# Page gathers spread thinner over the token tiles, feature tiles paced by attention units, output weights loaded by column halves

## The chip, the cores and the metric

The kernel runs on one core of one Trainium2 chip. TensorE (PE) multiplies matrices, VectorE (DVE), ScalarE (ACT) and GpSimd (POOL) work on tiles in on-chip memory, and SyncE (SP) does little but issue DMAs. ACT issues DMAs too, on a queue of its own: a DMA that ACT issues stands in ACT's instruction order like a cast does, and whatever stands behind it waits until the issue is through. The metric is the device time of one execution in microseconds (us); lower is better.

## The reference

One decoder layer on 1024 prompt tokens and 8 sample tokens, model width 1024. A combined projection feeds two groups of heads: a chunked gMLP (u, v, gate z_a; 512 wide) and a sparse attention (8 query heads, 2 key/value heads, three branches: compressed, selected, sliding window). Their outputs are concatenated, projected once, added to the input and normalised. For the sample tokens, part of the keys and values come out of paged caches.

```python
z = jnp.einsum('btd,de->bte', rms_norm(x, norm_g), w_in)
u, v, z_a, q, kc, vc, ks, vs, kw, vw, g, z_b = jnp.split(z, offs, axis=-1)
a_out, vn = gmlp_branch(u, v, z_a, ...)             # u * (W_s @ layer_norm(v) + b) * silu(z_a)
pages = lambda c: c[page_table].reshape(Bn, past, N_KV, HEAD_DIM)    # sample tokens only
kc_full = jnp.concatenate([pages(ck_cmp), kc], 1)   # likewise vc, ks, vs
kcc, starts = compress(kc_full, w_ck, pe_ck)
o_b = nsa_core(q, pos, gates, kcc, vcc, c_end, kb, vb, kw_all, vw_all, kwpos)
mix = jnp.concatenate([a_out, o_b * silu(z_b)], -1)
y = rms_norm(x + jnp.einsum('bte,ed->btd', mix, w_out), final_g)
```

## The kernel before

All large products are made with operands split into a high and a low part (`hi`, a cast by ACT, and `lo`, a subtraction by DVE or POOL), so that one product is three matmuls: hi·hi, lo·hi and hi·lo. Helper `f_mm` and its like issue them all from line L45, which is why the rows are told apart by tile names and not by lines.

The program runs in stages on one core:

- 0 to 60 us: the input is read and normalised, and the first three feature tiles are made. A **feature tile** (PSUM tile `pf`) is 128 columns of the projection for all 1032 tokens, 8 slices of the model width times 3 column thirds times 3 products.
- 60 to 97 us: the four **query tiles** (t = 0 to 3), also `pf`. Each takes two weight tiles, loaded by SP into `wst` (from `wF`), cast to `whi` by ACT (L143) and subtracted to `wlo` (L144). The weights of t = 0 and 1 are in the list `q_first`, made ahead; those of t = 2 and 3 are asked for inside the loop with `f_weights(8 + t)`.
- 97 to 180 us: eight **token tiles of v** (`ptv`), with the gate of the gMLP (`pg`).
- 180 to 226 us: eight token tiles of **keys** (`pta`), 199 to 243 us: eight token tiles of **values** (`ptb`), each evacuated by ACT from PSUM into `ka`, `kvc` or `vb`, `kvc`, then cast to `k` or `v`. PE then transposes `kvc` (`pct`) for the compressed branch.
- 246 to 365 us: compression (`Xh`, `pc`) and the sample tokens' attention, between which the remaining nine feature tiles are strewn as filler work.
- 365 to 735 us: 32 **attention units**, one for each of eight query blocks qb, two key/value heads and two halves. A unit has scores `S`, softmax on DVE, ACT and POOL (`Pl`, `Pw`), transposes `pt`, casts `th` and `tl` of the probabilities, and products with the values into `o`. For qb 0 to 3 the filler beside them is the rest of the feature tiles; for qb 4 to 7 it is the output projection `pout`, which needs `woh` and `wol`, the high and low parts of the output weights. These two reuse the memory of `xh` and `xl`, the input's parts, so they can be loaded only after the last feature tile.

What sets the order. A scheduler orders each engine's instructions by a time model of its own; `tc.high_priority(FILL)` with a negative FILL marks filler that yields to everything else, and `tc.issue_after(x)` keeps what it wraps behind instruction x. Each engine then runs its instructions in that fixed order.

Function `early(t, behind)` is called once for each of the 24 token tiles t: 0 to 7 are those of v, 8 to 15 of keys, 16 to 23 of values. It puts side work on ACT's DMA queue behind that tile's evacuation. For t under 16 it gathers one of 16 pages of `cg` (for compression, copied from cache to scratch memory), loads one half slice of the output weights (`wost`), casts it (`wohi`) and has POOL subtract (`wolo`), whose result the next call stores to `wol_d`. For t from 16 on it gathers two of 16 pages of `kg` (for selected attention). `cg` has the layout (o k) p c, with 256 rows of 128 elements on both sides; `kg` splits each row of the page in two, from "o p (k c)" to "(o k) p c" with k = 2. Each page is 128 KB.

After qb 3 is written (`od`), the output weights are loaded: SP issues eight loads of 128x1024 (L1189, pool `wop` with 7 buffers) and two of `wol` (L1193), and ACT casts eight slices of `woh` (L1190). `fg`, the last norm's weights, takes over the memory of `RS`.

Of the kernel before, what the change touches and what calls it, by code (L numbers as in the profile page):

```python
# [12 lines left out]
P = 128  # L13
# [26 lines left out]
def trunk(tc, io, outs):  # L40
# [7 lines left out]
    with ExitStack() as top:  # L48
# [251 lines left out]
        wp = wp_ctx.enter_context(tc.tile_pool(name="wp", bufs=9, reuse_waits="tile"))  # L300
        wr_ctx = ExitStack()
# [9 lines left out]
        W.update(pool=wp, rp=wr, raw=4, behind=sy.dma_start(Sq, io["Sq"]))  # L311
# [27 lines left out]
        for t in range(4):  # L339
            if t:  # L340
                qF = f_tiles(t + 1)
            wts = f_weights(8 + t) if t > 1 else q_first[t]
# [33 lines left out]

        def early(t, behind):
            half, k = t % 2, t // 2
            cs_ = slice(half * 512, half * 512 + 512)
            with tc.issue_after(behind.ins):  # L380
                if wo_low:
                    s.dma_start(*wo_low.pop())
                if t < 16:
                    s.dma_start(cg[:, :, t, :], io["cA"][bass.ds(prow[t], 1)].rearrange("o k p c -> (o k) p c"))
                    st = wo.tile([P, 512], F32, tag="wost", name="wost")
                    s.dma_start(st, io["w_out"][k, :, cs_])
# [5 lines left out]
                else:  # L392
                    for j in range(2 * t - 32, 2 * t - 30):
                        s.dma_start(kg[:, :, j, :],  # L394
                                    io["cB"][bass.ds(prow[j], 1)].rearrange("o p (k c) -> (o k) p c", k=2))
# [203 lines left out]
        def feature_tiles(bank):  # L599
# [5 lines left out]
            for n, (what, i, _) in enumerate(todo):  # L605
# [5 lines left out]
                for j in range(3):  # L611
                    ps = bank()("pf")[:, 0:CH]
                    for k in range(KT):
                        hi, lo = wts[k // 4]
                        c = (k % 4) * P
                        with tc.high_priority(FILL):
                            at_bank[1] = f_mm(hi[:, c:c + P], lo[:, c:c + P], [ps], k, (j,))
# [25 lines left out]
        at_bank = [0, None]  # L643
        banks = [ps_s, ps_b]
# [506 lines left out]
        for i, (qb, h, tp) in enumerate(todo):  # L1151
            units = [n_values(q) + 2 for q, _, _ in todo[i:] if (q < EARLY) == (qb < EARLY)]
# [25 lines left out]
            if qb == EARLY - 1:  # L1178
# [3 lines left out]
                fg = xp.tile([P, D], F32, tag="row", name="fg")  # L1182
# [3 lines left out]
                wop = wo_ctx.enter_context(tc.tile_pool(name="wop", bufs=7, side="right", reuse_waits="tile"))  # L1186
                for k in range(KT):
                    st = wop.tile([P, D], F32, tag="wost", name="wost")
                    sy.dma_start(st, io["w_out"][k])  # L1189
                    s.copy(woh[:, k, :], st)  # L1190
                    if k == 6:
                        for half in range(2):
                            sy.dma_start(f32(wol[:, :, half * 512:half * 512 + 512]), wol_d[half])  # L1193
# [130 lines left out]
```

## Time and profile before

| | us |
|---|---|
| median of 3 runs | 749.3 (747.53 to 750.55) |
| profiled execution | 745.39 |
| its span, first to last instruction | 743.6 |
| PE busy within the span | 683.4 |
| DVE busy | 510.6 |
| ACT busy | 383.0 |
| POOL busy | 294.5 |

The profiled execution took 1.8 us more than its span and is 3.9 us under the median of the runs. "Busy" leaves out DMA-issuing instructions, so ACT's 383.0 us do not hold the time its queue spends on issues; those are named ACTq in the rows (SPq for SyncE's). Matmul records overlap, so a matmul's pace is read from the distance of starts, or from the number that starts in a stretch.

The granted TensorE clock is a column of the stage table, 1.00 for full speed and 0.50 for half. It was 0.968 in the mean over the span.

### The profile page before, as it was taken

To read this page: it belongs to the slowest core of one execution; us is meant where nothing else is said; L and a number is where in the kernel's file an instruction comes from. 1 tells how busy PE (TensorE), PEld (TensorE's weight loads), DVE (VectorE), ACT (ScalarE), POOL (GpSimd) and SP (SyncE) were. 2 spreads that over 40 slices of the span, in tenths; PEclk is the share of its full clock that TensorE was granted. 3 is DMA by queue.
4 is the path that set the end of the run, shared out by engine and by line. 5 is a ranking of instruction groups with operands and counts; after the bars stand their busy time and mean duration, and the time that the engine had idled before them with its cause. 6 is when DMAs were issued, how large, how long until landed. Compare 5 with 4: busy or idle time off the path is not lost.

```text
span 743.6 us, 12579 instructions
## 1 busy us (share of the span) xinstructions
PE 683.4 (92%) x4186; PEld 628.1 (84%) x4186; DVE 510.6 (69%) x1470; ACT 383.0 (52%) x898; POOL 294.5 (40%) x282
## 2 busy tenths in 40 slices
PE   8998999998899256999999999979999999999994
PEld 6997988898799256898899999757989988988993
DVE  5836894798561135843299998968788789878743
ACT  7613422232453135512278777798567676676631
POOL 0034133646132104152322343558565565556421
PEclk9999899999999768999999999999999999999998
DMA  9333655333873245254542212955031121212011
GB/s 323 111 113 143 181 143 166 104 93 117 253 217 111 78 147 176 99 196 154 145 117 66 86 53 93 332 211 176 26 113 44 59 57 61 71 57 86 15 57 57
DMA packets 67945, 91.29 MB, mean 123 GB/s; under 512 B 5744, under 2 KB 45280, under 8 KB 67080
## 3 DMA queue, kind: packets, MB, share of 16 engines
q1 hardware_dynamic: 54344, 75.48, 31.7%
q10 hardware_dynamic: 13376, 12.85, 5.4%
q0 software_dynamic: 160, 2.15, 0.9%
q8 instruction: 33, 0.54, 0.3%
q14 instruction: 32, 0.26, 0.1%
HBM read 67.85 MB, written 28.91 MB: 130 GB/s over the span
## 4 chain that ended last, share of the span: by engine, by line
PE 54%; DVE 12%; DMA 11%; issue 7%; ACTq 6%; ACT 5%; POOL 3%; SPq 1%; POOLq 0%; DVEq 0%
PE pf L45 15%; PE pout L45 11%; PE o L45 8%; PE S L45 7%; PE pt L966 7%; ACTq L394 4%; DMA kg<-in_cB 2%; DMA zd<-z 2%; DMA wost<-in_w_out 1%; PE ptb L45 1%; PE po L45 1%; DVE sp L445 1%; PE pouts L45 1%; POOL vt L469 1%; PE pA L45 1%
## 5 line engine op out<-in xcount | busy, mean ns | idle before, releaser
L970 DVE TENSOR_TENSOR tl<-pt,th 128x512 fp32r<-128x512 f32 (+1 forms) x160 | 100.7, 643 | 25.6 <-ACT th L969 24.9
L45 PE MATMUL pf<-xh,whi 128*128 128x344 f32 x384 | 109.7, 332 | 4.8 <-ACT whi L143 2.5
L45 PE MATMUL pf<-xl,whi 128*128 128x344 f32 x384 | 111.1, 329 | 0.0
L45 PE MATMUL pf<-xh,wlo 128*128 128x344 f32 x384 | 110.1, 328 | 1.0 <-DVE wlo L144 1.0
L969 ACT CAST th<-pt 128x512 fp32r<-128x512 f32 (+1 forms) x160 | 84.8, 550 | 30.0 <-PE pt L966 27.2
L943 POOL TENSOR_TENSOR Pw<-Pw,r 128x640 f32<-128x640 f32 (+3 forms) x112 | 76.2, 699 | 42.8 <-DVE r L937 17.2
L45 PE MATMUL pout<-woh,mix 128*128 128x512 f32 (+1 forms) x272 | 86.4, 383 | 1.8 <-ACT mix L1003 1.8
L943 POOL TENSOR_TENSOR Pl<-Pl,r 128x384 f32<-128x384 f32 (+5 forms) x36 | 49.0, 1362 | 89.6 <-DVE r L937 33.9
L45 PEld LDWEIGHTS pf<-xh,whi 128*128 128x128 f32 x384 | 71.2, 195 | 6.7 <-ACT whi L143 3.2
L45 PE MATMUL o<-th,v 128*128 128x256 f32 x264 | 73.3, 298 | 3.0 <-ACT th L969 2.1
L45 PEld LDWEIGHTS pf<-xl,whi 128*128 128x128 f32 x384 | 71.8, 195 | 1.2 <-issue 1.0
L45 PEld LDWEIGHTS pf<-xh,wlo 128*128 128x128 f32 x384 | 71.2, 194 | 1.8 <-DVE wlo L144 1.4
L45 PE MATMUL o<-tl,v 128*128 128x256 f32 x264 | 69.3, 288 | 0.8 <-DVE tl L970 0.7
L45 PEld LDWEIGHTS pout<-woh,mix 128*128 128x128 f32 x272 | 49.9, 188 | 10.5 <-ACT mix L1003 2.0
L889 ACT ACTIVATE Pl<-Pl,nmx 128x128 f32<-128x128 f32 (+7 forms) x64 | 49.8, 778 | 15.1 <-DVE nmx L885 12.9
L45 PE MATMUL S<-kwS,q 128*128 128x384 f32 (+2 forms) x224 | 54.9, 336 | 2.9 <-DVE nmx L885 1.9
L929 ACT ACTIVATE Pw<-Pw,nmx 128x640 f32<-128x640 f32 (+4 forms) x64 | 44.5, 696 | 22.5 <-DVE nmx L921 20.6
L45 PEld LDWEIGHTS o<-th,v 128*128 128x128 f32 x264 | 49.8, 189 | 6.3 <-ACT th L969 2.9
L45 PE MATMUL S<-ksS,q 128*128 128x384 f32 (+5 forms) x192 | 53.5, 363 | 1.1 <-DVE nmx L885 0.7
L45 PEld LDWEIGHTS o<-tl,v 128*128 128x128 f32 x264 | 49.9, 189 | 3.8 <-DVE tl L970 2.6
L45 PE MATMUL pout<-wol,mix 128*128 128x512 f32 (+1 forms) x136 | 52.1, 384 | 0.0
L143 ACT CAST whi<-wst 128x512 fp32r<-128x512 f32 (+2 forms) x50 | 28.4, 587 | 41.1 <-DMA wst<-in_wTv 11.9
(338 smaller groups left out, 1674.3 us busy)
## 6 DMA issues: line engine op xcount, KB each, us to landing
q<-qd SPq DMA_DIRECT2D x32, 256.0 KB
wst<-in_wF SPq DMA_DIRECT2D x26, 256.0 KB
raw<-in_xw SPq DMA_DIRECT2D x7, 708.0 KB
wost<-in_w_out ACTq DMA_DIRECT2D x16, 256.0 KB
wol_d<-wolo ACTq DMA_DIRECT2D x16, 256.0 KB
wol<-wol_d SPq DMA_DIRECT2D x2, 2048.0 KB
wost<-in_w_out SPq DMA_DIRECT2D x8, 512.0 KB
xt<-in_x_prompt SPq DMA_DIRECT2D x8, 512.0 KB
```

Of the source, the lines that this page charges most:

```text
L45: return pe.matmul(out, lhsT, rhs, start=start, stop=stop, skip_group_check=True)
L143: s.copy(hi[:, :n], st[:, :n])
L394: s.dma_start(kg[:, :, j, :], io["cB"][bass.ds(prow[j], 1)].rearrange("o p (k c) -> (o k) p c", k=2))
L445: v.tensor_tensor(sp[rows, 2 * half:2 * half + 2, :], ps[rows].rearrange("p (a r t) -> p r a t", a=2, r=2)[:, r], bsb[rows, 2 * half:2 * h ...
L469: g.tensor_tensor(vt[:n, :], vt[:n, :], lng[:n, :], op=ALU.mult)
L889: s.activation(Pl[:, 0:L], Pl[:, 0:L], AF.Exp, bias=nmx[:, 0:1], scale=-1.0, accum_out=sums[:, 1:2])
L929: s.activation(Pw[:, 0:nw], Pw[:, 0:nw], AF.Exp, bias=nmx[:, 1:2], scale=-1.0, accum_out=sums[:, 2:3])
L943: g.tensor_tensor(t_[:, a:b], t_[:, a:b], r[:, j:j + 1].to_broadcast((P, b - a)), op=ALU.mult)
L966: pe.transpose(pt[:, ci * 256 + e * P:ci * 256 + (e + 1) * P], src[e][:, col:col + P], ident)
L969: s.copy(th[:, :n], pt[:, :n])
L970: v.tensor_tensor(tl[:, :n], pt[:, :n], f32(th[:, :n]), op=ALU.subtract)
```

## The change

The diff has four parts.

1. **Query weights.** The pool `wp` is put to use as soon as it exists, and `f_weights(10)` and `f_weights(11)`, the weights of the query tiles t = 2 and 3, are asked for there and put in `q_first`. They use the older raw buffers (two of them) and no longer wait behind the load of `Sq`.
2. **Gathers.** `early` issues two pages of `cg` for each of the eight tiles of v, and one page of `kg` for each of the 16 tiles of keys and values. Before, it was one `cg` for each of 16 tiles and two `kg` for each of the eight value tiles. The side work on output weights stays with t under 16.
3. **Pacing.** The filler matmuls of a feature tile that are given to unit i (from i = 1 on) are kept behind the last `o` matmul of unit i - 1.
4. **Output weights by column halves.** Sixteen loads of 128x512 (pool of 10 buffers) and 16 casts of 512 columns take the place of eight of 1024. `wol`'s first half is asked for after the first eight, the second after two more; `fg` is allocated and loaded after them.

```diff
@@ wp pool, ahead of the query tiles
+        W.update(pool=wp)
+        q_first += [f_weights(10), f_weights(11)]
...
-        W.update(pool=wp, rp=wr, raw=4, behind=sy.dma_start(Sq, io["Sq"]))
+        W.update(rp=wr, raw=4, behind=sy.dma_start(Sq, io["Sq"]))
...
-            wts = f_weights(8 + t) if t > 1 else q_first[t]
+            wts = q_first[t]
...
@@ early(t, behind)
+        def gather(n):
+            if n < 16:
+                s.dma_start(cg[:, :, n, :], io["cA"][bass.ds(prow[n], 1)].rearrange("o k p c -> (o k) p c"))
+            else:
+                s.dma_start(kg[:, :, n - 16, :],
+                            io["cB"][bass.ds(prow[n - 16], 1)].rearrange("o p (k c) -> (o k) p c", k=2))
...
                 if wo_low:
                     s.dma_start(*wo_low.pop())
+                if t < 8:
+                    gather(2 * t)
+                    gather(2 * t + 1)
+                else:
+                    gather(8 + t)
                 if t < 16:
-                    s.dma_start(cg[:, :, t, :], io["cA"][bass.ds(prow[t], 1)].rearrange("o k p c -> (o k) p c"))
...
-                else:
-                    for j in range(2 * t - 32, 2 * t - 30):
-                        s.dma_start(kg[:, :, j, :],
-                                    io["cB"][bass.ds(prow[j], 1)].rearrange("o p (k c) -> (o k) p c", k=2))
@@ feature_tiles
-                        with tc.high_priority(FILL):
+                        with tc.high_priority(FILL), paced():
...
+        pace = []
+
+        def paced():
+            return tc.issue_after(pace[0]) if pace else ExitStack()
...
         for i, (qb, h, tp) in enumerate(todo):
+            if i:
+                pace[:] = [blocks[todo[i - 1][0]]["last"].ins]
@@ after qb 3
-                fg = xp.tile([P, D], F32, tag="row", name="fg")
...
-                wop = wo_ctx.enter_context(tc.tile_pool(name="wop", bufs=7, side="right", reuse_waits="tile"))
-                for k in range(KT):
-                    st = wop.tile([P, D], F32, tag="wost", name="wost")
-                    sy.dma_start(st, io["w_out"][k])
-                    s.copy(woh[:, k, :], st)
-                    if k == 6:
-                        for half in range(2):
-                            sy.dma_start(f32(wol[:, :, half * 512:half * 512 + 512]), wol_d[half])
+                wop = wo_ctx.enter_context(tc.tile_pool(name="wop", bufs=10, side="right", reuse_waits="tile"))
+                for half in range(2):
+                    cs_ = slice(half * 512, half * 512 + 512)
+                    for k in range(KT):
+                        st = wop.tile([P, 512], F32, tag="wost", name="wost")
+                        sy.dma_start(st, io["w_out"][k, :, cs_])
+                        s.copy(woh[:, k, cs_], st)
+                        if k == (7 if half == 0 else 1):
+                            sy.dma_start(f32(wol[:, :, cs_]), wol_d[half])
                 wo_ctx.close()
+                fg = xp.tile([P, D], F32, tag="row", name="fg")
                 sy.dma_start(fg, io["final_g"].partition_broadcast(P))
```

How the instructions stand. On ACT, at the last value tiles (`vb` and `kvc` are the evacuations of a tile, `v` its cast, `kg` the gather), before:

```order
L568 ACTIVATE vb<-ptb,rs 128x256
L569 ACTIVATE kvc<-ptb,rs 128x128
L576 CAST v_1910<-vb 128x4x64
L394 ISA
L394 DMA kg<-in_cB 256x1x128
L394 ISA
L394 DMA kg<-in_cB 256x1x128
L568 ACTIVATE vb<-ptb,rs 128x256
L569 ACTIVATE kvc<-ptb,rs 128x128
L576 CAST v_1910<-vb 128x4x64
```

and on ACT in the middle of the key tiles, after (`ka` is a key tile's evacuation, `ksS` a copy of the transposed keys):

```order
L536 ACTIVATE kvc<-pta,rs 128x128
L143 CAST whi<-wst 128x408
L552 CAST ksS<-pkt 128x2x128
L546 CAST k_2112<-ka 128x4x64
L383 ISA
L383 DMA kg<-in_cB 256x1x128
L389 DMA wol_d<-wolo 128x512
L401 CAST wohi<-wost 128x512
L552 CAST ksS<-pkt 128x2x128
L398 DMA wost<-in_w_out 128x512
L546 CAST k_2165<-ka 128x4x64
```

A `kg` gather moved from behind each value tile to behind a key tile, into the same queue as the loads and stores of the output weights; behind a value tile one is left of two.

On PE, where the attention units begin (`S` are the first units' scores, `pf` filler), before:

```order
L45 MATMUL pf<-xh,wlo 128x344
L45 MATMUL S<-ksS,q_3685 128x128 x2
L45 MATMUL S<-kwS,q_3685 128x192 x2
L45 MATMUL S<-ksS,q_3685 128x128 x2
L45 MATMUL pf<-xh,whi 128x344
L45 MATMUL pf<-xl,whi 128x344
L45 MATMUL pf<-xh,wlo 128x344
```

and the same place on PE after, from the eleventh row of scores on:

```order
L45 MATMUL S<-ksS,q_3859 128x128 x2
L978 MATMUL pt<-ident,Pl 128x128
L978 MATMUL pt<-ident,Pw 128x128
L45 MATMUL S<-kwS,q_3859 128x192 x2
L978 MATMUL pt<-ident,Pl 128x128
L978 MATMUL pt<-ident,Pw 128x128 x3
L45 MATMUL S<-ksS,q_3859 128x128 x2
L45 MATMUL S<-kwS,q_3859 128x192 x2
L45 MATMUL S<-ksS,q_3859 128x128 x2
L978 MATMUL pt<-ident,Pl 128x128
L45 MATMUL o<-th,v_1918 128x256
L45 MATMUL o<-tl,v_1918 128x256
```

The filler between the first scores is gone: 22 score matmuls stand in a row before the first transpose, and the next filler stands behind the sixth product `o`. Further on, the last `pf` stood behind the 120th product `o` before and stands behind the 174th now; the first `pout` stood behind the 236th and stands behind the 258th.

## Rows read from the trace of the kernel before

**Rows 1.** Page: busy engines (first row), and the chain that ended last, by line.

```profile
PE 683.4 (92%) x4186; PEld 628.1 (84%) x4186; DVE 510.6 (69%) x1470; ACT 383.0 (52%) x898; POOL 294.5 (40%) x282
PE pf L45 15%; PE pout L45 11%; PE o L45 8%; PE S L45 7%; PE pt L966 7%; ACTq L394 4%; DMA kg<-in_cB 2%; DMA zd<-z 2%; DMA wost<-in_w_out 1%; PE ptb L45 1%; PE po L45 1%; DVE sp L445 1%; PE pouts L45 1%; POOL vt L469 1%; PE pA L45 1%
```

**Rows 2.** What PE waited for, 40 to 300 us: us in total, times, longest.

```profile
PE pct L691 <- DVE kccs L586: 21.5, 1, 21.5
PE pc L45 <- ACT Xh L685: 5.9, 1, 5.9
PE pf L45 <- ACT whi L143: 2.5, 1, 2.5
...
PE pf L45 <- DVE wlo L144: 1.0, 1, 1.0
```

**Rows 3.** ACT, 254 to 275 us: start, duration (us), instruction, idle before it and its releaser.

```profile
259.89 0.47 ACT L568 ACTIVATE vb<-ptb,rs 128x256 f32<-128x256 f32 x1 [5.33 <-issue]
...
260.53 5.63 ACTq L394 DMA_DIRECT2D kg<-in_cB  x2
266.34 0.47 ACT L568 ACTIVATE vb<-ptb,rs 128x256 f32<-128x256 f32 x1 [5.43 <-issue]
```

**Rows 4.** Gather issues on ACT's queue by tile: ns min/median/max, first and last start.

```profile
L394 ACTq DMA_DIRECT2D kg<-in_cB x16: 621/2940/4131, 220.0 to 269.3; - x16
L384 ACTq DMA_DIRECT2D cg<-in_cA x16: 502/516/1012, 122.4 to 215.5; - x16
L386 ACTq DMA_DIRECT2D wost<-in_w_out x16: 334/608/1512, 123.1 to 219.4; - x16
```

**Rows 5.** PE, 240 to 292 us: as in rows 3.

```profile
268.04 1.12 PE L691 MATMUL pct<-ident,kvc 128*128 128x128 f32 x4 [21.54 <-DVE kccs L586]
...
285.63 0.69 PE L45 MATMUL pc<-Xh,w 128*128 128x386 f32 x1 [5.85 <-ACT Xh L685]
```

**Rows 6.** Stages: from:to, length, busy (instructions) per engine, granted PE clock, DMA share, GB/s.

```profile
72.00:105.00 33.00, 32.00 (x171) 30.11 (x171) 29.49 (x30) 10.29 (x18) 11.48 (x4) 0.90 0.59 158
...
120.00:180.00 60.00, 58.72 (x322) 52.39 (x320) 48.23 (x127) 16.96 (x30) 35.55 (x30) 1.00 0.33 103
180.00:200.00 20.00, 18.59 (x112) 17.24 (x110) 10.56 (x35) 6.52 (x18) 4.79 (x5) 1.00 0.71 231
...
256.00:262.00 6.00, 0.00 (x0) 0.00 (x0) 0.67 (x2) 1.02 (x3) 0.00 (x0) 0.50 0.21 62
...
268.00:274.00 6.00, 5.96 (x25) 5.96 (x26) 0.26 (x1) 0.80 (x2) 0.00 (x0) 0.58 0.61 175
274.00:280.00 6.00, 5.78 (x37) 5.49 (x35) 5.36 (x13) 3.87 (x11) 0.00 (x0) 1.00 0.69 218
...
286.00:290.00 4.00, 4.00 (x15) 4.00 (x15) 2.72 (x5) 1.44 (x4) 2.67 (x3) 0.50 0.49 156
...
482.00:495.00 13.00, 9.46 (x54) 6.85 (x53) 8.65 (x34) 12.75 (x25) 5.44 (x6) 1.00 0.81 304
```

**Rows 7.** ACT around the first key tiles, as in rows 3.

```profile
188.14 0.41 ACT L538 CAST k<-ka 128x256 fp32r<-128x256 f32 x1 [6.25 <-DVE ka L512]
```

**Rows 8.** Two longer stages, columns as in rows 6.

```profile
460.00:517.00 57.00, 49.13 (x319) 40.77 (x318) 48.77 (x179) 49.01 (x119) 33.18 (x37) 0.97 0.72 248
517.00:735.00 218.00, 215.06 (x1337) 193.46 (x1335) 167.77 (x507) 136.13 (x297) 112.72 (x96) 1.00 0.19 60
```

**Rows 9.** Casts of the output weights by line: ns min/median/max, first and last start.

```profile
L1190 ACT CAST woh<-wost x8: 1032/1050/1062, 482.2 to 497.9; 128x1024 fp32r<-128x1024 f32 x8
L389 ACT CAST wohi<-wost x16: 608/620/667, 126.4 to 227.5; 128x512 fp32r<-128x512 f32 x16
```

**Rows 10.** PE at the first attention unit, as in rows 3.

```profile
369.96 0.41 PE L45 MATMUL S<-ksS,q 128*128 128x128 f32 x2 [0.16 <-DMA q<-qd]
...
381.78 0.30 PE L45 MATMUL o<-th,v 128*128 128x256 f32 x1
```

**Rows 11.** Filler tile `pf` alone at the first attention unit: PE, PEld, DVE, ACT, clock.

```profile
370.00:382.00 12.00, 8.42 (x48) 7.49 (x48) 0.97 (x3) 0.00 (x0) 1.00 0.49 132
```

More of the change, by code (lines that the diff above doesn't have):

```diff
@@ L375, in trunk @@
         wo_low = []
+        def gather(n):
[4 more added lines that the diff above has]
+                            io["cB"][bass.ds(prow[n - 16], 1)].rearrange("o p (k c) -> (o k) p c", k=2))
         def early(t, behind):
-            half, k = t % 2, t // 2
-            cs_ = slice(half * 512, half * 512 + 512)
             with tc.issue_after(behind.ins):
@@ L382, in early @@
                     s.dma_start(*wo_low.pop())
+                if t < 8:
[3 more added lines that the diff above has]
+                    gather(8 + t)
                 if t < 16:
-                    s.dma_start(cg[:, :, t, :], io["cA"][bass.ds(prow[t], 1)].rearrange("o k p c -> (o k) p c"))
+                    half, k = t % 2, t // 2
                     st = wo.tile([P, 512], F32, tag="wost", name="wost")
-                    s.dma_start(st, io["w_out"][k, :, cs_])
+                    s.dma_start(st, io["w_out"][k, :, half * 512:half * 512 + 512])
                     hi = wo.tile([P, 512], F32R, tag="wohi", bufs=1, name="wohi")
```

## The prediction

> **What bounds the kernel now.** I read the page first: PE is busy for 683.4 of 743.6 us [rows 1], so the 60 us in which it idles, and the stretches in which it runs at half its clock, are all that a change of order can win. The chain that ended last is mostly PE's, but ACT's queue stands in it with 4% for one line, L394, and the transfer of `kg` with 2% [rows 1]: some 30 and 15 us behind gathers. Next I read what PE waited for. One wait stands out: 21.5 us ahead of the transposes `pct`, then 5.9 us for `Xh`, then 2.5 and 1.0 us for query weights [rows 2]. The long one is put down to `kccs` on DVE, which is only what came last; ACT's timeline shows what it is. ACT needs about a microsecond for a value tile, and then is held for 5.63 us by two `kg` issues before it may evacuate the next, so that the last value tiles are 6.45 us apart (259.89, 266.34) [rows 3]. A `kg` issue takes 2.94 us in the median, a `cg` issue, of the same size, 0.52 us [rows 4]. PE, done with the values' matmuls, stands still from 246.5 to 268.04 [rows 5], at a granted clock of 0.50 [rows 6]; it starts again at the low one of its two levels (1.2 GHz; the full one is 2.4) and has 0.58 in the mean from 268 to 274, which costs 6 x (1 - 0.58) = 2.5 us more. From 286 to 290, after the wait for `Xh`, it is 0.50 again: 2.0 us [rows 6].
>
> Last I read the stages of the attention units. PE is nearly full in them; it idles 57 - 49.1 = 7.9 us between filler and projection (460 to 517 us) and 218 - 215.1 = 2.9 us after [rows 8].
>
> **The gathers.** The change leaves one `kg` behind a value tile and puts the other eight behind the key tiles, and the last eight `cg` go to the tiles of v. There they cost 8 x 0.52 = 4.1 us of ACT in a stage in which it is busy for 17.0 of 60 us and PE for 58.7 [rows 4, 6]: hidden, so nothing; if ACT were late there, PE would pay at most those 4.1 us, and I give it no more than a share of the range. In the key stage each tile puts 2.94 in place of 0.52 us on ACT's queue, 19.4 us in eight tiles, and the first `kg` can go near 188 us, behind the first cast `k` [rows 7], instead of at 220.0 [rows 4]. Queued behind it on ACT are the tile's weight load, its store, and the next tile's evacuation, for which PE waits when its PSUM buffers are used up.
>
> Best end: the whole wait goes and the clock stays up, 21.5 + 2.5 = 24 us. Worst end: gathers still run one after another and ACT does nothing beside them, so that only ACT's free time ahead of 220.0 is won. ACT was busy 6.52 us of the 20 from 180 [rows 6], at that rate 13 of 40; eight `cg`, `wost` and `wol_d` issues (the last taken like a `wost`) add 8 x (0.52 + 0.61 + 0.61) = 14 us, which leaves 13; of these I count 10, since some of the free time lies ahead of 188. Between them: 16 gathers need 16 x 2.94 = 47 us, and from 188 to 246.5 there are 58, but they share these with 16 issues for output weights. One `kg` for a tile (46 us for eight key tiles: 5.75 each) is less than a tile's time, two were more. So I take it that most of the stall goes and that one or two gathers are still in the way at the end, 4 us: 21.5 - 4 = **17.5 us**, from 10 to 24, the better clock after it counted only in the upper end.
>
> The price of a gather is where a rule bears on this. The row shows 2940 against 516 ns for equal bytes [rows 4], and a DMA share of 0.21 while ACT's queue is full of them [rows 6]. The Trainium skill ("DMA: Bandwidth & Descriptors", section "Why a DMA increments its semaphore by 16 and not by 1") says that a transfer is shared among as many engines as the largest number up to 16 that divides the slowest dimension of both sides; with the outer two of `kg` that would be two engines, and with the 256 rows of `cg` sixteen. The trace agrees so far: the longer issues are those of that shape. By the rule a gather does not get cheaper by standing elsewhere, which speaks against the change and makes the first rival's 740 us; had the gathers been slow only because they came in pairs, the sum would be the second rival's 714.
>
> **The wait behind it.** `Xh` is cast from `cg` once it is loaded back, and the load is issued by SP only after the value tiles' stores. With the gathers ended earlier, that load meets less traffic, while the filler that PE has until then (up to 285.63 - 5.85 = 279.8) stays. Ends: nothing, or 5.85 + 2.0 = 7.9 us [rows 5, 6]. Nothing in the rows decides it; I take the middle, **4 us**.
>
> **The query weights.** They take the waits of 2.5 and 1.0 us [rows 2] and the low clock behind them, 33 x (1 - 0.90) = 3.3 us [rows 6]: 6.8 at most. The weights of t = 2 now stand in front of SP's other loads, those of t = 3 still come behind two loads for v, and a cast of ACT is put ahead of the copies of the first query tile. Below nothing only if the v tiles' weights come later, for which PE would wait just as long; I take half, **3.5 us**, from 0 to 6.8.
>
> **Pacing and the output weights.** Here PE's work is the same and only its gaps move. At the first unit it is 11.8 us from the first score to the first product [rows 10], and 48 filler matmuls lie in it [rows 11], at 0.156 us each (37 in 5.78 us [rows 6]) 7.5 us of work. After the change no filler may stand there, so up to 7.5 us of idle time come up. In return the gap without filler shrinks from 116 products `o` to 84 (the 174th to the 258th), which takes 32/116 of its 7.9 us, 2.2 us [rows 8]. The casts of output weights are 16 x 0.62 = 9.9 us for 8 x 1.05 = 8.4 [rows 9], 1.5 us more on an engine that was busy for 12.75 of 13 us there [rows 6]. Worst: -7.5 + 2.2 - 1.5 = -6.8. Best: the filler put off fills most of both late gaps, 7.9 + 2.9 less part of 7.5, +5. I take **-4 us**, nearer to the worst, since the missing filler is written in the order and the gain is not. The loads in smaller pieces and the later `fg` I cost at nothing: the 84 products cover them (some 0.5 us each); without that cover the first `pout` would wait, within the rival that ends slower.
>
> **The sum.** 17.5 + 4 + 3.5 - 4 = 21.0 us. The span goes from 743.6 to 722.6, the execution from 745.4 to 724.4. The runs' median was 3.9 us above the profiled execution, so 749.3 - 21.0 = 728.3, **728 us**.
>
> **The rivals.**
>
> *The block only moves.* The key stage takes over what the value stage gives. For it: the equal price of a gather wherever it stands [rows 4], and a key tile's sum on ACT: 2.94 + 0.61 + 0.61 of issues and some 2.8 of evacuations and casts (five at 0.36 to 0.47 [rows 3, 7] and one at 0.62 [rows 9]) make 7 us, more than the 5.75 that PE takes. Against it: PE had 1.4 us of idle time in 20 there [rows 6], and issues may overlap casts. Then the gathers give 10, `Xh` nothing, the query weights 3.5, the units -4: 749.3 - 9.5 = 740. Chance 0.18.
>
> *Everything goes.* 22 to 24 from the gathers, 6 from `Xh`, 5 from the queries, nothing lost in the units: about 35 us, 714. For it: gathers are fewer per tile than a tile lasts. Chance 0.15.
>
> *Pacing starves the units* (slower). Fifteen units hold their filler back until the last product of the one before. If PE then waits for softmax in each of them as it may in the first, where 7.5 us of cover go [rows 11], the other parts' 25 us are used up from 25/15 = 1.7 us per unit on. At 2 us, 30 us are lost: 749.3 - 25 + 30 = 754. Against it: DVE and ACT have each unit's scores one unit ahead, so the filler of unit i lies beside the softmax of i + 1. Chance 0.07.
>
> *The gathers were not the cause.* `pct` waits for something else that ends at 268, and only the queries and the units change: 749.3 - 3.5 + 4 = 750. Against it: the issues fill ACT between the late tiles without a gap [rows 3]. Chance 0.05.
>
> **How the numbers follow.** The forecast, 728 (720 to 737), has the remaining 0.55. The range reaches to the second rival on one side and to just above the first on the other, 714 to 742, and leaves out the last two cases and the tails. Differences under 0.5% (3.7 us) are about what a measurement of this kernel can tell from no change. Faster by more: 0.55 + 0.18 + 0.15 = 0.88; within: 0.05; slower: 0.07.
>
> **What would show it.** Right: the wait of `pct` falls to a few us and `pct` starts near 250; `kg` issues start near 188 and end before 250; the evacuations `vb` follow the matmuls; the wait for query weights at 70 us is gone, and the mean clock from 72 to 105 rises above 0.90; the filler's last matmul comes later, and the stretch without filler has under 7.9 us idle. Wrong: waits of PE for `ka`, `k` or `wohi` in the key stage (the first rival), waits of `pt` or `o` for `th`, `Pl` or `Pw` in every early unit (the third), `pct` still after 260 (the fourth).

## The result, and the profile after

The changed kernel takes 744.4 us (15 runs, 740.4 to 746.2) where the kernel before takes 748.35 us (15 runs, 746.2 to 752.05): a ratio of 0.994 with a 95% interval of 0.9923 to 0.9957, 4.5 us faster within 3.2 to 5.8. The forecast was 728 with a range of 714 to 742. The sign was right, the size was not, and the range missed the time by 2.4 us.

First the page of the changed kernel, PE's row and the chain by line, to be read beside [rows 1]:

```profile
PE 693.6 (93%) x4186; PEld 636.6 (86%) x4186; DVE 509.1 (69%) x1470; ACT 383.0 (52%) x906; POOL 293.1 (39%) x282
PE pf L45 15%; PE pout L45 12%; PE o L45 10%; PE S L45 9%; PE pt L978 8%; PE ptv L45 3%; PE pta L45 3%; DMA wst<-in_wF 2%; PE pg L45 2%; PE pc L45 2%; DVE wlo L144 2%; DMA wost<-in_w_out 1%; DMA wst<-in_w_c 1%; PE po L45 1%; DMA kg<-in_cB 1%
```

The line of the gathers' issues is no longer in the list; their transfer still has 1%. But PE is busy for 10 us longer with the same 4186 matmuls: more of its work runs at the lower clock (in the kernel before, the longest low stretch fell into idle time). So "idle" alone doesn't tell what was won; half clock has to be added. The next two views give both, by stage (from:to, length, then busy time of PE, PEld, DVE, ACT and POOL with the instructions, granted clock, DMA share, GB/s), for the kernel before (460 to 735 us is in [rows 8])

```profile
60.00:105.00 45.00, 41.36 (x229) 38.93 (x228) 36.74 (x38) 14.17 (x26) 17.47 (x6) 0.92 0.58 171
105.00:180.00 75.00, 73.72 (x386) 64.55 (x384) 55.82 (x155) 19.91 (x34) 37.33 (x31) 1.00 0.40 118
180.00:226.00 46.00, 42.64 (x251) 40.51 (x249) 25.87 (x77) 20.63 (x55) 11.46 (x10) 1.00 0.69 216
226.00:268.00 42.00, 20.50 (x115) 19.93 (x114) 6.38 (x16) 9.01 (x23) 6.57 (x5) 0.78 0.29 90
268.00:300.00 32.00, 26.11 (x136) 25.80 (x137) 17.00 (x28) 16.04 (x24) 8.80 (x8) 0.81 0.64 201
300.00:365.00 65.00, 63.33 (x400) 57.48 (x399) 30.25 (x62) 17.20 (x43) 21.25 (x20) 1.00 0.36 127
365.00:460.00 95.00, 94.02 (x677) 92.50 (x678) 83.76 (x349) 69.48 (x232) 34.35 (x54) 1.00 0.30 86
```

and for the changed one:

```profile
60.00:105.00 45.00, 45.00 (x257) 42.09 (x257) 39.82 (x40) 14.35 (x27) 17.57 (x6) 1.00 0.53 155
105.00:180.00 75.00, 70.49 (x361) 61.61 (x360) 51.13 (x153) 18.29 (x32) 35.84 (x31) 0.95 0.44 129
180.00:226.00 46.00, 36.14 (x195) 33.34 (x194) 23.33 (x73) 18.80 (x48) 11.02 (x10) 0.93 0.60 188
226.00:268.00 42.00, 37.54 (x209) 36.90 (x208) 11.07 (x28) 14.13 (x37) 7.74 (x6) 0.96 0.51 157
268.00:300.00 32.00, 26.32 (x156) 25.90 (x155) 25.24 (x38) 18.18 (x29) 9.85 (x9) 0.89 0.41 137
300.00:365.00 65.00, 60.60 (x376) 54.54 (x376) 26.33 (x79) 16.22 (x51) 22.49 (x23) 0.98 0.46 151
365.00:460.00 95.00, 94.42 (x662) 91.45 (x662) 84.40 (x350) 73.35 (x238) 34.68 (x56) 0.96 0.24 71
460.00:517.00 57.00, 51.45 (x336) 45.54 (x335) 47.21 (x165) 45.44 (x114) 28.29 (x32) 0.96 0.71 223
517.00:735.00 218.00, 213.48 (x1297) 190.18 (x1296) 159.89 (x488) 133.14 (x290) 115.11 (x96) 0.99 0.20 65
```

PE's loss in a stage is its idle time plus its busy time times what the clock lacks (for 226 to 268 us of the kernel before only the idle time, since the low clock fell into it):

| stage, us | before | after | difference |
|---|---|---|---|
| 60-105, queries | 3.6 + 3.3 = 6.9 | 0 | -6.9 |
| 105-180, v tiles | 1.3 | 4.5 + 3.5 = 8.0 | +6.7 |
| 180-226, keys and values | 3.4 | 9.9 + 2.5 = 12.4 | +9.0 |
| 226-268, values, `pct` | 21.5 | 4.5 + 1.5 = 6.0 | -15.5 |
| 268-300, `Xh`, `pc` | 5.9 + 5.0 = 10.9 | 5.7 + 2.9 = 8.6 | -2.3 |
| 300-365 | 1.7 | 4.4 + 1.2 = 5.6 | +3.9 |
| 365-460, first units | 1.0 | 0.6 + 3.8 = 4.4 | +3.4 |
| 460-517 | 7.9 + 1.5 = 9.4 | 5.6 + 2.1 = 7.7 | -1.7 |
| 517-735, `pout` | 2.9 | 4.5 + 2.1 = 6.6 | +3.7 |

The stages are cut at fixed times, so they hold slightly different work in the two kernels. The two profiled executions also lie only 1.0 us apart (745.39 and 744.38 us), so the table shows where time was won and lost, and not how much the whole won. The pattern is plain. Both large gains are there, and a new loss follows each: 6.7 us in the v tiles behind the queries' 6.9, and 9.0 us in the key stage ahead of the gathers' 15.5. The stages from 300 us on lose another 9.3 us together, most of it to the lower clock.

What PE waited for in the changed kernel, the longest first (us in total, times, longest), answers [rows 2]:

```profile
PE pkt L551 <- DVE k L548: 7.0, 3, 4.6
PE pc L45 <- ACT Xh L697: 5.7, 1, 5.7
PE pct L703 <- DVE kccs L594: 4.5, 1, 4.5
PE pg L45 <- ACT vh L482: 3.3, 1, 3.3
...
PE pta L45 <- ACT kvc L536: 2.6, 1, 2.6
```

The wait of 21.5 us is 4.5 now and the two for query weights are gone. New are 9.6 us in the key stage (`pkt` waits for DVE's half of the keys, a subtraction behind ACT's cast, and `pta` for an evacuation) and 3.3 us in the v tiles (`pg` waits for `vh`). The wait for `Xh` is what it was.

### The profile page after: what moved, and what is told of

Its sections match the earlier page's. It is cut to its first block, busy times and chain, and to the rows that moved or that the text cites. A ratio compares the mean times of both kernels' runs of the same rounds, so it can differ in the third digit from the quotient of the medians.

```text
span 742.6 us, 12587 instructions
## 1 busy us (share of the span) xinstructions
PE 693.6 (93%) x4186; PEld 636.6 (86%) x4186; DVE 509.1 (69%) x1470; ACT 383.0 (52%) x906; POOL 293.1 (39%) x282
## 4 chain that ended last, share of the span: by engine, by line
PE 67%; DVE 9%; DMA 9%; issue 6%; ACT 4%; ACTq 2%; POOL 1%; SPq 0%; POOLq 0%; DVEq 0%
PE pf L45 15%; PE pout L45 12%; PE o L45 10%; PE S L45 9%; PE pt L978 8%; PE ptv L45 3%; PE pta L45 3%; DMA wst<-in_wF 2%; PE pg L45 2%; PE pc L45 2%; DVE wlo L144 2%; DMA wost<-in_w_out 1%; DMA wst<-in_w_c 1%; PE po L45 1%; DMA kg<-in_cB 1%
## 5 line engine op out<-in xcount | busy, mean ns | idle before, releaser
L45 PE MATMUL pout<-woh,mix 128*128 128x512 f32 (+1 forms) x272 | 88.3, 391 | 2.2 <-ACT mix L1015 1.8
L45 PE MATMUL o<-th,v 128*128 128x256 f32 x264 | 75.9, 307 | 2.6 <-DVE oT L991 2.2
L978 PE MATMUL pt<-ident,Pw 128*128 128x128 f32 x304 | 50.0, 276 | 0.4
```

The costliest lines, as they stand in the source:

```text
L45: return pe.matmul(out, lhsT, rhs, start=start, stop=stop, skip_group_check=True)
L978: pe.transpose(pt[:, ci * 256 + e * P:ci * 256 + (e + 1) * P], src[e][:, col:col + P], ident)
```

## What the gathers do in the key stage

The gathers' issues, beside [rows 4] (ns min/median/max, first and last start):

```profile
L383 ACTq DMA_DIRECT2D kg<-in_cB x16: 604/626/3277, 186.2 to 258.1; - x16
```

Taken alone this looks like a full success: 626 ns in place of 2940. But 15 steps from 186.2 to 258.1 us are 4.8 us per gather, where they were (269.3 - 220.0) / 15 = 3.3 us apart before. The new places alone don't ask for this: cheap gathers in the same places come 3.3 us apart (last of the experiments on a gather's price). ACT's timeline in the key stage shows where the time has gone (start, us, instruction, idle before it and releaser):

```profile
190.19 0.65 ACTq L383 DMA_DIRECT2D kg<-in_cB  x1
190.88 5.16 ACTq L398 DMA_DIRECT2D wost<-in_w_out  x1
196.09 0.62 ACT L401 CAST wohi<-wost 128x512 fp32r<-128x512 f32 x1 [5.64 <-DMA wost<-in_w_out]
196.62 0.47 ACT L535 ACTIVATE ka<-pta,rs 128x256 f32<-128x256 f32 x1
196.98 0.36 ACT L536 ACTIVATE kvc<-pta,rs 128x128 f32<-128x128 f32 x1
```

It is the instruction behind the gather that is held now: the load of an output-weight slice takes 5.16 us to issue, and its cast and the evacuations `ka` and `kvc` stand behind it. PE pays for it in the same place (PE's timeline of the changed kernel, columns as before):

```profile
197.39 0.45 PE L45 MATMUL pta<-whi,xsS 128*128 128x384 f32 x1 [2.60 <-ACT kvc L536]
...
221.71 0.56 PE L551 MATMUL pkt<-identr,k 128*128 128x128 f32 x4 [4.56 <-DVE k L548]
...
259.60 1.11 PE L703 MATMUL pct<-ident,kvc 128*128 128x128 f32 x4 [4.46 <-DVE kccs L594]
```

`pct` resumes at 259.6 us, where the forecast's 17.5 us make 250.5 and the kernel before had 268.0.

## Experiments: each part alone

**Queries alone.** The first part on the kernel before:

```diff
+        W.update(pool=wp)
+        q_first += [f_weights(10), f_weights(11)]
...
-            wts = f_weights(8 + t) if t > 1 else q_first[t]
+            wts = q_first[t]
```

> The kernel before with the first part of the change alone (weights of the query tiles t = 2 and 3 asked for early). From the two traces: between 60 and 105 us PE lost 6.9 us before (idle plus half clock) and nothing after, but from 105 to 180 us it lost 1.3 before and 7.5 after. Theory A (the early weights are worth what the queries waited, and the loss in the v tiles comes from the second cg gather): about -7 us, with the first v matmul near 90 us and pg not waiting for vh. Theory B (the early weights and their casts only push the v tiles back): -2 to +1 us, with PE waiting ahead of pg near 120 us here too.

Measured: 747.6 us, ratio 0.9981 (0.9958 to 1.0005), so -1.4 us within -3.1 and +0.4. The first v matmul starts at 91.8 us instead of 97.4, but the last one ends at 151.6 instead of 151.4. PE waits ahead of `pg` as in the changed kernel, though each v tile still has one `cg` gather: theory B. The loss in the v tiles comes with the early weights, and not with the second `cg`.

**Gathers alone.** The second part on the kernel before:

```diff
+                if t < 8:
+                    gather(2 * t)
+                    gather(2 * t + 1)
+                else:
+                    gather(8 + t)
```

> The kernel before with the second part alone (two cg per v tile, one kg per key and value tile). The traces give 7.7 us gained from 180 to the transposes pct and 2.4 behind them, and 6.2 us lost in the v tiles. Theory A (the loss in the v tiles is the gathers'): -3 to -5 us. Theory B (it is the early query weights'): about -10 us. Theory C, that of the forecast (most of the stall goes): -17 to -20 us; it falls if the key stage shows PE waiting for k or kvc as in the changed kernel, about 7 to 10 us there.

Measured: 738.95 us, ratio 0.9886 (0.9853 to 0.992), -8.5 us within -11 and -6. This lies next to B's 10 and beyond A's 5, and it excludes C, the forecast's: `pkt` waits for 6.9 us here too, `pct` for 4.7. Its stage of v tiles has 1.8 us of idle time at full clock, against 1.3 before, so the second `cg` costs next to nothing there.

**Pacing alone.** The third part on the kernel before:

```diff
-                        with tc.high_priority(FILL):
+                        with tc.high_priority(FILL), paced():
```

> The kernel before with the third part alone (filler of a unit kept behind the last product of the unit before). Theory A (missing filler in the first units leaves gaps and lowers the clock, as the trace of after shows with 6.7 us lost from 360 to 465 against 1.0): +3 to +6 us. Theory B (the gaps are only moved, and the gap ahead of the output projection shrinks by as much): -1 to +1 us. The forecast had -5 to +2 for this part with part four.

Measured: 749.14 us, ratio 1.0017 (0.9994 to 1.004), so +1.3 us within -0.4 and +3.0: no change that can be told, with theory A's 3 to 6 at or beyond its end. PE's first score and first product in this kernel, beside [rows 10]:

```profile
370.15 0.41 PE L45 MATMUL S<-ksS,q 128*128 128x128 f32 x2 [1.25 <-DMA q<-qd]
...
376.74 0.36 PE L45 MATMUL o<-th,v 128*128 128x256 f32 x1
```

From one to the other it is 6.6 us, where it was 11.8: the filler had not only covered the wait for softmax, it had stood in the way of it too. The gap ahead of the projection in this kernel, beside [rows 8]:

```profile
460.00:517.00 57.00, 54.68 (x384) 49.93 (x382) 52.04 (x191) 45.88 (x117) 27.87 (x32) 1.00 0.57 199
```

PE's idle time there falls from 7.9 to 2.3 us, while the stages on either side lose 2.3 and 3.1 us more (365 to 460, 517 to 735): the gaps moved, as theory B had it.

**Halves alone.** The fourth part on the kernel before:

```diff
-                    sy.dma_start(st, io["w_out"][k])
-                    s.copy(woh[:, k, :], st)
+                        sy.dma_start(st, io["w_out"][k, :, cs_])
+                        s.copy(woh[:, k, cs_], st)
```

> The kernel before with the fourth part alone (output weights loaded and cast by column halves, fg later). Theory A (the later start of the projection and 16 casts of 0.62 us cost what the finer loads give): -1 to +2 us. Theory B (the halves let the projection start earlier): -3 to -5 us, first pout ahead of 515 us. Theory C (SP's issues, held at the 16 loads, delay q and mix): +3 us or more.

Measured: 747.9 us, ratio 0.9998 (0.9976 to 1.0019): no change, theory A. The first `pout` starts at 518.6 us, 1.5 later than before.

## Experiments: what makes a gather slow

**The wide gather.** One edit on the kernel before, the shape of the copy:

```diff
-                        s.dma_start(kg[:, :, j, :],
-                                    io["cB"][bass.ds(prow[j], 1)].rearrange("o p (k c) -> (o k) p c", k=2))
+                        s.dma_start(kg[:, :, j, :].rearrange("k p c -> p k c"),
+                                io["cB"][bass.ds(prow[j], 1)].rearrange("o p (k c) -> (o p) k c", k=2))
```

> The kernel before with one edit: a kg gather is written with the page's 128 rows as the outer dimension on both sides and the two halves inside, instead of the two halves outside; same bytes, same pieces of 512 bytes, same place in the program, still two behind each value tile. Theory A (a gather is slow because its outer dimension of two puts it on few engines, as the Trainium skill, page DMA: Bandwidth & Descriptors, has it; the trace had 2940 ns against 516 for cg): the kg issues fall to about 0.5 to 0.6 us, the wait of pct (21.5 us) goes, and the time falls by 20 to 28 us. Theory B (the price is in the gather's source or the traffic, not its shape): issues stay near 2.9 us and the time within 2 us of before.

Measured: 718.74 us, ratio 0.96 (0.9552 to 0.9647), 30 us faster and 26 us under the changed kernel. The issues in this kernel:

```profile
L394 ACTq DMA_DIRECT2D kg<-in_cB x16: 542/542/591, 218.4 to 240.0; - x16
```

and the stage that held the 21.5 us, columns as in the stages above:

```profile
226.00:268.00 42.00, 40.19 (x238) 39.27 (x238) 22.26 (x42) 21.81 (x40) 13.79 (x10) 1.00 0.69 219
```

The gathers end at 240 us while they still stand two behind each value tile, and PE is busy for 40.2 of 42 us at full clock (20.5 before). PE's wait for `Xh` falls to 0.7 us as well.

**The other reading.** The wide form also changes the order of the 256 pieces. To tell order from engines, the row-by-row form was cut into 122 and 6 rows:

```diff
+                        for a, b in ((0, 122), (122, 128)):
+                            s.dma_start(kg[:, a:b, j, :].rearrange("k p c -> p k c"),
+                                        io["cB"][bass.ds(prow[j], 1)][:, a:b].rearrange("o p (k c) -> (o p) k c", k=2))
```

> The kernel before with the kg gather written row by row as in the wide form, but cut into 122 and 6 rows (122 has 2 as its largest divisor up to 16). Theory A (the number of engines sets the price, and the outer dimension sets that number): the gather of 122 rows is as slow as the old form, issues of 2.5 to 3.5 us, pct waits 15 to 25 us, the time is within 5 us of before. Theory B (the order of the pieces, rows inside halves, makes it slow): issues of 0.5 to 0.7 us for both and the time within 5 us of the wide form's 719.

Measured: 757.79 us, ratio 1.013 (1.0094 to 1.0166): 9.7 us slower than before, outside theory A's 5, and 39 us above theory B. Theory A missed in two more numbers: the 32 issues take 0.80 us in the median and up to 5.06, not 2.5 to 3.5, and `pct` waits 10.5 us for `kccs`, not 15 to 25. But the gathers as a whole are no cheaper: they are issued from 222.2 to 279.7 us, 57 us, where the old form took 49 and the wide one 22. That the number of issues makes the rest slower is likely and not shown. ACT's timeline in this kernel, between late value tiles (issues shown together):

```profile
260.67 5.11 ACTq L395 DMA_DIRECT2D kg<-in_cB  x3
...
265.96 9.92 ACTq L395 DMA_DIRECT2D kg<-in_cB  x4
```

The order of the pieces is that of the fast form, and the price is that of the slow one. What ACT's queue (q10) moved from 240 to 260 us, when almost only gathers were on it (packets, MB, share of 16 engines), in the kernel before:

```profile
q10 hardware_dynamic: 1516, 0.77, 12.7%
```

and in the one with 122 and 6 rows:

```profile
q10 hardware_dynamic: 1611, 0.80, 13.3%
```

12.7% of 16 engines are 2.0 in the mean, 13.3% are 2.1. The Trainium skill ("DMA: Bandwidth & Descriptors", section "Why a DMA increments its semaphore by 16 and not by 1") has a transfer use as many engines as the largest number up to 16 that divides the slowest dimension of both sides, and by it 2 and 122 both give two. Both traces agree.

**The wide gather in the changed kernel.** The same edit, in `gather(n)`:

```diff
-                s.dma_start(kg[:, :, n - 16, :],
-                            io["cB"][bass.ds(prow[n - 16], 1)].rearrange("o p (k c) -> (o k) p c", k=2))
+                s.dma_start(kg[:, :, n - 16, :].rearrange("k p c -> p k c"),
+                                io["cB"][bass.ds(prow[n - 16], 1)].rearrange("o p (k c) -> (o p) k c", k=2))
```

> The changed kernel with the same edit of the kg gather. Theory A (the spread-out gathers hold the output weights' loads and stores behind them on ACT's queue, and PE's waits for k and kvc in the key stage are those): the 5 us issues of wost behind kg go, the key stage loses under 4 us in place of some 14, pct starts near 248, and the time is 14 to 22 us under that of the changed kernel. Theory B (the key stage is slow for another reason, such as the wTb or wost transfers): 0 to 5 us.

Measured: 720.52 us, ratio 0.962 (0.9583 to 0.9658), 24 us under the changed kernel: theory A, somewhat above its upper end. The issues of the output weights and the key stage, first of the changed kernel (its key stage stands above),

```profile
L398 ACTq DMA_DIRECT2D wost<-in_w_out x16: 334/582/5158, 121.7 to 228.9; - x16
```

then of this one:

```profile
L398 ACTq DMA_DIRECT2D wost<-in_w_out x16: 334/553/668, 122.3 to 215.8; - x16
```

and this one's key stage and gathers:

```profile
180.00:226.00 46.00, 45.77 (x271) 44.22 (x270) 29.04 (x84) 25.97 (x67) 17.05 (x14) 1.00 0.79 246
L383 ACTq DMA_DIRECT2D kg<-in_cB x16: 542/558/1032, 187.0 to 237.0; - x16
```

The issue of 5.16 us has gone with nothing else changed, and so has the key stage's loss (12.4 to 0.2 us). With cheap gathers these runs can't tell the old places (718.7 us) from the new ones with the other three parts (720.5).

## Experiments: how the parts go together

**One part undone.** In each of these four kernels the lines of one part of the change are as in the kernel before. The changed kernel without the pacing:

```diff
-                        with tc.high_priority(FILL), paced():
+                        with tc.high_priority(FILL):
```

> The changed kernel without the pacing. The parts alone gave -9.4 (gathers), about -1 (queries), +0.8 (pacing) and -0.5 us (halves), which would make -10; together they gave -4.5. Theory A (pacing costs more together with the late first pout of the halves, since the same filler is missed twice): 3 to 6 us faster than the changed kernel, near 740. Theory B (the gain is lost where queries and gathers meet, in the v tiles): within 1.5 us of the changed kernel.

Measured: 742.2 us, ratio to the kernel before 0.9922 (0.9896 to 0.9948). Without the early query weights:

```diff
-            wts = q_first[t]
+            wts = f_weights(8 + t) if t > 1 else q_first[t]
```

> The changed kernel without the early query weights. Theory A (the early weights give nothing, because the v tiles end at the same time with and without them, 151 us in the first experiment): within 1.5 us of the changed kernel. Theory B (with two cg per v tile on ACT's queue the early weights disturb the v stage): 3 to 6 us faster, with PE's wait for vh ahead of pg gone.

Measured: 742.2 us, ratio 0.9923 (0.9897 to 0.9949). Without the gathers:

```diff
-                if t < 8:
-                    gather(2 * t)
-                    gather(2 * t + 1)
-                else:
-                    gather(8 + t)
```

> The changed kernel without the second part (queries early, pacing and halves together, gathers as before). Alone the three gave about -1, +0.8 and -0.5 us, and the gathers -9.4. Theory A (the parts add): within 1.5 us of before, so that the gathers' share is eaten where the parts meet. Theory B (the three together cost what the whole change lacks): +3 to +6 us over before.

Measured: 750.0 us, ratio 1.0038 (1.0018 to 1.0057). Without the halves:

```diff
-                        s.copy(woh[:, k, cs_], st)
+                    s.copy(woh[:, k, :], st)
```

> The changed kernel with the output weights loaded as before (8 loads of 128x1024). Theory A (halves are worth nothing either way): within 1.5 us of the changed kernel. Theory B (pacing and halves both shift the projection to a later place and cost together): 3 to 5 us faster.

Measured: 741.27 us, ratio 0.9916 (0.9887 to 0.9945).

Each of the three smaller parts, left out of the changed kernel, gives some 1 to 2 us back (1.3, 1.3 and 1.8 by the ratios to the kernel before), within intervals that reach to nothing. So the "within 1.5 us" theories of the first two fit best, and the third lies between its two. The three together cost 2.8 us (1.3 to 4.3), between the two theories of that run. The gathers' 8.5 less these 2.8 make 5.7, against 4.5 measured, within the intervals. That the three cost more together than alone (-1.4 + 1.3 - 0.2 = -0.3) is likely but not shown: the singles' intervals are each 3.2 to 3.5 us wide. Single traces point to the first attention units, 365 to 460 us, which lose 1.0 us before, 4.4 in the changed kernel, 3.3 with the pacing alone and 1.5 in the changed kernel without it. Which parts disturb each other stays open.

**Wide gather with queries and halves.** The kernel before with the wide gather's edit and parts one and four of the change:

```diff
+                        s.dma_start(kg[:, :, j, :].rearrange("k p c -> p k c"),
...
+            wts = q_first[t]
...
+                        s.copy(woh[:, k, cs_], st)
```

> The kernel before with the wide kg gather, early query weights and the column halves, without spreading the gathers and without pacing. Theory A (these two parts move nothing once the gathers are cheap, as alone): within 2 us of the wide form's 718.7. Theory B (their few us count when nothing waits behind gathers): 713 to 716.

Measured: 717.56 us, ratio 0.9599 (0.9567 to 0.963): theory A, nothing to tell from the wide gather alone.

## Experiments: where the queries' gain goes

In the first experiment PE comes to the v tiles 5.5 us earlier and is held there. `pg` waits for `vh`, and ACT's timeline has `vh` where it was. Before, on ACT and then on PE:

```profile
116.38 0.51 ACT L143 CAST whi<-wst 128x384 fp32r<-128x384 f32 x1 [7.00 <-DMA wst<-in_wTa]
122.29 0.62 ACT L474 CAST vh<-vt 128x512 fp32r<-128x512 f32 x1 [5.39 <-POOL vt L470]
...
124.94 0.40 PE L45 MATMUL pg<-wsh,vh 128*128 128x256 f32 x2
```

With the early query weights:

```profile
116.37 0.51 ACT L143 CAST whi<-wst 128x384 fp32r<-128x384 f32 x1 [8.15 <-DMA wst<-in_wTa]
122.20 0.62 ACT L476 CAST vh<-vt 128x512 fp32r<-128x512 f32 x1 [5.32 <-POOL vt L472]
...
122.87 0.50 PE L45 MATMUL pg<-wsh,vh 128*128 128x256 f32 x2 [3.29 <-ACT vh L476]
```

and on DVE, in the same kernel, what stands ahead of it:

```profile
116.92 0.56 DVE L144 TENSOR_TENSOR wlo<-wst,whi 128x384 fp32r<-128x384 f32 x1 [5.14 <-ACT whi L143]
117.39 0.22 DVE L103 SCALAR_TENSOR_TENSOR rv<-r_a,r_y 128x1 f32<-128x1 f32 x2
117.58 1.00 DVE L470 TENSOR_SCALAR vt<-vt,mv,rv 128x512 f32<-128x512 f32 x2
```

A subtraction for the first key weight stands in DVE's order ahead of the last steps of v's normalisation. Its load is issued behind the last rotated query's store, and its cast starts at 116.4 us in both traces, though PE is 5.5 us earlier in the second. `vt`, then POOL's two steps, then `vh` wait behind it. (In the traces of the changed kernel and of the later kernels with early query weights PE comes to the v tiles 7 to 8 us earlier than before and this cast 2 to 3 us earlier, so the load follows PE in part; PE still waits about 3 us for `vh`.) To test this, that one subtraction was kept behind `vl` of the second v tile:

```diff
+            with tc.issue_after(after.ins) if after else ExitStack():
+                e.tensor_tensor(lo[:, :n], st[:, :n], f32(hi[:, :n]), op=ALU.subtract)
...
-            return [load_w(src[k], cols) for k in range(KT)]
+            return [load_w(src[k], cols, after=W["vl"] if k == 0 else None) for k in range(KT)]
...
+                vl_in = v.tensor_tensor(vl, vt, f32(vh), op=ALU.subtract)
+                if i == 1:
+                    W["vl"] = vl_in
```

> The first experiment (before with early query weights alone) with one more edit: the subtraction wlo of the first key weight is kept on DVE behind the products' input vl of the second v tile, instead of ahead of the normalisation's last steps. In the first experiment's trace that subtraction waits 5.14 us for a cast that waits for a load issued behind the last query's store, and the normalisation of v tiles 0 and 1 stands behind it on DVE; vh starts at 122.20 there and at 122.29 before. Theory A (that order gives the query part's gain back): vh starts near 118, PE's wait of 3.3 us ahead of pg goes, the last v matmul ends near 147 in place of 151.6, and the time is 3 to 6 us under the first experiment's (741 to 744). Theory B (the v stage is held by DVE or POOL as a whole): last v matmul at 150 or later, time within 1.5 us of the first experiment's.

Measured: 743.46 us, ratio 0.9931 (0.9906 to 0.9956), 4.1 us under the first experiment's median (3.7 by the ratios): theory A. `vh` in this kernel:

```profile
114.12 0.62 ACT L477 CAST vh<-vt 128x512 fp32r<-128x512 f32 x1
```

It starts 8 us earlier (2.6 of them since this profile came to the v tiles earlier), PE's wait for it is 0.2 us, and the last v matmul ends at 144.1 us. So the query part, with this order, is worth 5.2 us (3.3 to 7.0). Then the same on the wide form with queries and halves:

> The same edit on the kernel with the wide gather, early query weights and halves (717.6 us). Theory A: 3 to 6 us faster, 712 to 715. Theory B: within 1.5 us.

Measured: 711.58 us, ratio 0.9503 (0.9475 to 0.9531), 6.0 us under the wide form with queries and halves: theory A, 0.4 us past its end. It is the fastest kernel here, 37 us under the kernel before and 33 under the changed one. Some 30 of the 37 come from the shape of one copy, and 6 from the place of one subtraction on top of the early query weights. Its page:

```profile
PE 675.9 (96%) x4186; PEld 623.0 (88%) x4186; DVE 509.0 (72%) x1470; ACT 381.7 (54%) x906; POOL 293.0 (41%) x282
```

## Why the prediction went wrong

**What bounds the kernel: right.** The long wait of `pct` is that of ACT behind the `kg` issues, and not of `kccs` on DVE. With cheap gathers it is gone, which also drops the fourth rival.

**The gathers: the step that failed.** The forecast took 17.5 us, and 4 for `Xh`; alone this part gave 8.5 with both (6 to 11), in the middle below the 10 that were its worst end. The failing step is "One `kg` for a tile (46 us for eight key tiles: 5.75 each) is less than a tile's time, two were more. So I take it that most of the stall goes". It set one gather of 2.94 us against a tile of 5.75 us, and both sides were wrong. The tile is shorter: PE makes value tiles from 199 us on, so the 46 us hold more than eight tiles, and with cheap gathers, one behind each of the 16 tiles, they came 3.3 us apart. The queue's work is longer: what shares it in that stage, a load and a store of 256 KB for each key tile, was named but counted at what their issues took while no gather was ahead of them, 0.61 us each; behind a gather an issue takes up to 5.16 us. Even 2.94 and two of 0.61 make 4.2 for a key tile, more than 3.3. The gathers came 4.8 us apart, and from 186.2 us on 15 such steps end at 258, not by the 246.5 up to which the forecast had room for them.

The first rival had the mechanism and the price of the gathers (10 us). About half of what its 740 us missed of the measured 744.4 is the other parts, which it counted at 0.5 us of cost and which cost 2.8 together; that the gathers alone came to 738.95 is partly chance. The text had the rule that makes this rival likely, and gave it 0.18.

**The wait for `Xh`: none of the 4 us.** It is 5.7 us after 5.9. The last gather is issued at 258.1 us and SP issues the load at 262.3; before, that was 269.3 and 273.6, the same 4 us apart. With cheap gathers the wait is 0.7 us in the old places and 2.5 in the new ones, so it hangs on the gathers' price more than on their place. How they hold it up is not shown.

**The query weights: the waits went, the time did not.** The 6.9 us of waits and low clock are zero after, as the upper end had it, but alone they give 1.4 us (nothing to 3.1) where 3.5 was taken. The forecast looked for a cost at the v tiles' weights; the limit was `vh`, tied to a load of key weights through one instruction on DVE. The trace of before showed it, since `vh` ended at 122.9 us and PE came to it only at 124.9: 2 us of slack for 5.5 us of gain.

**Pacing and output weights: -4 was too dark.** Alone they are +1.3 and -0.2 us, neither told from nothing. The step that failed is the 7.5 us of cover at the first unit: with the pacing alone the first product came 5 us sooner after the first score, PE's idle time from 360 to 380 us rose by 1.8 us (1.0 to 2.8) and not by 7.5, and the gap ahead of the projection was filled by 5.6 where 2.2 were taken.

**The sum.** 17.5 + 4 + 3.5 - 4 was 21; the parts alone give 8.5 + 1.4 - 1.3 + 0.2 = 8.8, and the whole gave 4.5. The queries, the pacing and the halves, which the forecast had at -0.5 us in all, cost 2.8 together. The third rival (starved units, 754 us) did not come, though the first units lose 3.4 us more than before.

**The trace's own tests.** The list of what would show it had a clock above 0.90 from 72 to 105 us, right (1.00), a `pct` wait of a few us, right (4.5), and `pct` near 250, wrong (259.6). It had `kg` issues from 188 us, right (186.2), ending before 250, wrong (258.1), and "waits of PE for `ka`, `k` or `wohi` in the key stage" for the first rival, which is what came (9.6 us).

## What to carry to other kernels

When DMAs hold up an engine, ask first why one of them is slow, and only then where to put it: moving 16 slow gathers won 8.5 us, and writing the same copy with its 128 rows outermost won 30. A slow transfer doesn't only delay its own issue: what stands behind it on the queue, and the engine that issues, pay for it in the new place, so count them there at their price behind a slow one. And a wait that is taken away on PE is worth little more than the slack of the next thing that PE waits for; look at what holds that one before counting the gain.

## What the runs showed of the hardware

Two copies of the same 128 KB in the same 512-byte pieces take 0.54 and 2.94 us to issue in the median, two behind each value tile, by the order of the dimensions alone. While the slow ones run, their queue keeps two of the 16 DMA engines' worth at work in the mean (12.7%). With a queue that has a slow copy ahead, an issue of another transfer, itself 0.58 us in the median, can hold its engine for 5.16 us; behind the fast copy the same issue takes 0.67 at most.
